# Seven products for every tile pair of the second MLP matrix, groups that alternate, and factors of twelve pairs made during the convolution

## The chip, the core and the metric

One core of one Trainium2 chip runs the whole program. The metric is the device time of one execution in microseconds (us). The kernel before took 1999.94 us, the median of three runs (1997.73 to 2001.57).

## What is computed

Two decoder layers over 256 tokens of width 2048, in float32. Layer 0 mixes with a gated short convolution, layer 1 with multi-head latent attention; each has a squared-ReLU MLP with 8192 hidden columns. The change lies in the MLP's second matrix, and uses the convolution's time.

In short:

```python
def short_conv_mixer(x, w_in, conv_w, w_out):
    gate_b, gate_c, u = jnp.split(x @ w_in, 3, axis=-1)
    y = causal_conv(gate_c * u, conv_w)          # width 3
    return (gate_b * y) @ w_out

def sq_relu_mlp(x, w1, w2):
    return jnp.square(jax.nn.relu(x @ w1)) @ w2

for layer in range(2):
    h = layer_norm(ALPHA * h + mix, ln_g[layer, 0], ln_b[layer, 0])
    h = layer_norm(ALPHA * h + sq_relu_mlp(h, mlp_w1[layer], mlp_w2[layer]),
                   ln_g[layer, 1], ln_b[layer, 1])
```

## The kernel before

**Numbers in two parts.** Every operand is kept as a high part, rounded to the matrix engine's float32r type, and a low part, the rest. `split` (L125 to L128) makes both from one 128x1024 tile: ScalarE casts the high part (L127), VectorE subtracts it from the source for the low part (L128). A product of two such operands is three matmuls: high by high, high by low, low by high (`dot`, L297 to L303).

**The stream of weights.** All weights pass once through a list `stream`, in the order in which the matrix engine needs them. `prepare` (L141) loads an entry from DRAM into one or more of five `raws` buffers of 128x1024 (`RAW`, on SyncE's queue, L138) and splits it into `hi` and `lo` tiles, of which there are eight each (`WA`). `take` (L183) hands an entry to the matrix engine and issues the preparation of what lies up to five steps ahead (`LOOK`). A plain entry is one step; an entry of the fast kind is three.

**The MLP.** It runs in eight passes `q` over 1024 hidden columns each. The first half of a pass (called W1 below) makes eight blocks of 128 hidden columns, `ps_u`, each from two 128x1024 tiles of the first matrix and 16 matmuls by the high part (512 columns) and 16 by the low part (256 columns), L215 and L219. The helper `hidden` brings each block through ReLU and square and splits it. The second half (W2) multiplies these eight hidden blocks by 1024 rows of the second matrix. Its 2048 output columns are two groups `g` of 1024; each group takes the hidden blocks in four pairs `j`, so a pass has eight (group, pair) steps.

**The fast kind.** In passes 1 to 6 (`FAST`) a pair is a 2x2 product of blocks (two halves of the tokens by two hidden blocks; two hidden blocks by two halves of the group's columns) in the form that needs seven products instead of eight. `FACTORS` (L340) lists them in order: 3, 1, 5, 7, 2, 6, 4. On the side of the hidden blocks the sums S1 to S4 are made by `form` (L703). On the side of the weights the entry loads two tiles, r1 (blocks 11 and 22) and r2 (21 and 12), and VectorE makes four derived blocks: T1 and T3 in one subtraction of 1024 columns (L162), T2 (L166) and T4 (L169) in one of 512 each. Then r1, the tile with T1 and T3, r2 (now 21 and T2), and T4 are split. T1 is used first by product 5, 21 by product 2, T4 by product 4. Beside the four output blocks of a group the form keeps four more sums (`OWN`: 1, 5, 7, 6), in `sums`; `fold` (L669) adds them into the outputs in the last pass.

**"sssp".** `MIXED` (L38) says that group 1, which always comes first, has three fast pairs and one plain pair: two plain entries of the stream, eight products, with an output sum of its own, "22". Group 0 has four fast pairs. So 57 products a pass.

**Sums between passes.** The sums of a group live in SBUF between uses. Group 1's eight are copied by ScalarE into PSUM banks during W1 (`resume` L626, through `resumed` L612) and back after W2's first group (`put_back` L616). Of group 0's seven, four are copied in before that group and back after it; for products 2, 6 and 4 it starts from nothing, and VectorE adds the result into SBUF (`keep`, L624), 128x512 each. In layer 1 passes 1 to 4 also add a block of the residual (`turn_residual`, two VectorE operations a pass).

**Order of the work.** The order of each engine's instructions is made by a planner that simulates the program at build time; each engine then runs its own list in that order and waits where a semaphore is not yet there. So the list can place preparation of weights between other work, but not change when something is late.

## Time and profile before

| what | value |
|---|---|
| median of three runs | 1999.94 us (1997.73 to 2001.57) |
| span of the profiled execution | 1994.9 us |
| matrix engine (PE) busy | 1987.7 us, 100% |
| VectorE (DVE) busy | 1709.4 us, 86% |
| ScalarE (ACT) busy | 1354.9 us, 68% |
| transfers | 385.85 MB, mean 193 GB/s |
| convolution, input products | until about 272 us |
| MLP of layer 0, passes 1 to 6 | 452.8 to 953.1 us |
| MLP of layer 1, passes 1 to 6 | 1395.4 to 1897.4 us |

The span runs from the first to the last instruction that the profiler records; the time of a run is some 5 us longer. A matmul's recorded duration overlaps the next one's, so the spacing of starts tells the pace. Busy time of VectorE in a stretch counts overlapping records once.

### The profile page before, as it was taken

The page shows a single profiled execution, that of the slowest core. Times are in us where ns is not written, and L with a number is a line of the kernel's source. Part 1 is how long each engine was busy: PE and PEld are TensorE (multiplying, and loading weights), DVE is VectorE, ACT ScalarE, POOL GpSimd, SP SyncE. Part 2 cuts the span into 40 slices and gives each one's busy share as a digit, 9 for nine tenths or more (in the row PEclk, how much of TensorE's full clock was granted, in tenths as well). Part 3 has the DMA queues.
Part 4 walks back from the last instruction along what each step waited for, and adds up shares of the span by engine and source line. Part 5 has one row for each costly group of instructions (what it writes and reads, how often), then busy time and mean ns, then how long its engine had stood idle before and what let it go on. Part 6 is the DMA issues. An engine that isn't in the chain of part 4 may idle for free.

```text
span 1994.9 us, 30180 instructions
## 1 busy us (share of the span) xinstructions
PE 1987.7 (100%) x11110; PEld 1737.2 (87%) x11110; DVE 1709.4 (86%) x2555; ACT 1354.9 (68%) x2154; POOL 2.3 (0%) x21
## 2 busy tenths in 40 slices
PE   9999999999999999999999999999999999999998
PEld 8888888988888888888889998898888888888886
DVE  8667667797999989989978988777899999999985
ACT  6444445586778778777756755558677787887772
POOL 0000000000000000000000000000000000000000
PEclk9999999999999999999999999999999999999999
DMA  8666666565657466574855543656464656656483
GB/s 318 205 191 187 190 190 190 179 193 157 212 170 251 148 216 221 177 243 147 281 171 159 170 140 123 201 180 195 146 233 155 232 161 220 222 178 233 150 269 130
DMA packets 106853, 385.85 MB, mean 193 GB/s; under 512 B 11857, under 2 KB 12625, under 8 KB 106449
## 3 DMA queue, kind: packets, MB, share of 16 engines
q1 hardware_dynamic: 106560, 383.79, 59.5%
q8 instruction: 87, 1.43, 0.3%
q14 instruction: 62, 0.50, 0.1%
q10 hardware_dynamic: 144, 0.13, 0.0%
HBM read 381.78 MB, written 2.10 MB: 192 GB/s over the span
## 4 chain that ended last, share of the span: by engine, by line
PE 98%; DVE 1%; ACT 1%; issue 0%; DVEq 0%; ACTq 0%
PE ps_u L215 20%; PE ps_l L215 13%; PE ps_u L219 10%; PE ps_l L219 7%; PE ps_f L300 4%; PE ps_f L303 4%; PE ps_f L302 4%; PE ps_r L303 4%; PE ps_r L302 4%; PE ps_r L300 4%; PE ps_d L300 2%; PE ps_d L302 2%; PE ps_d L303 2%; PE ps_w L249 2%; PE ps_w L248 2%; PE ps_w L247 2%
## 5 line engine op out<-in xcount | busy, mean ns | idle before, releaser
L128 DVE TENSOR_TENSOR lo<-raw,hi 128x1024 fp32r<-128x1024 f32 x710 | 861.8, 1220 | 190.6 <-ACT hi L127 119.9
L127 ACT CAST hi<-raw 128x1024 fp32r<-128x1024 f32 x710 | 741.8, 1051 | 247.4 <-PE ps_l L215 98.1
L215 PE MATMUL ps_u<-xhl,hi 128*128 128x512 f32 x1792 | 621.7, 392 | 0.0
L219 PE MATMUL ps_u<-xhl,lo 128*128 128x256 f32 x1792 | 498.2, 279 | 0.0
L215 PEld LDWEIGHTS ps_u<-xhl,hi 128*128 128x128 f32 x1792 | 334.5, 187 | 73.6 <-ACT acc L595 0.2
L219 PEld LDWEIGHTS ps_u<-xhl,lo 128*128 128x128 f32 x1792 | 338.1, 189 | 1.8
L215 PE MATMUL ps_l<-xhl_a,hi 128*128 128x512 f32 x704 | 244.1, 393 | 0.0
L219 PE MATMUL ps_l<-xhl_a,lo 128*128 128x256 f32 x704 | 195.4, 279 | 0.0
L215 PEld LDWEIGHTS ps_l<-xhl_a,hi 128*128 128x128 f32 x704 | 132.1, 188 | 29.9
L219 PEld LDWEIGHTS ps_l<-xhl_a,lo 128*128 128x128 f32 x704 | 131.9, 188 | 0.2
L127 ACT CAST hi_t<-raw_t 128x1024 fp32r<-128x1024 f32 x84 | 88.5, 1054 | 45.8 <-DVE raw_t L162 41.4
L162 DVE TENSOR_TENSOR raw_t<-raw,raw 128x1024 f32<-128x1024 f32 x84 | 102.3, 1218 | 1.8 <-DMA raw<-in_w2f_dram 1.5
L128 DVE TENSOR_TENSOR lo_t<-raw_t,hi_t 128x1024 fp32r<-128x1024 f32 x84 | 102.4, 1219 | 0.2
L718 ACT ACTIVATE fp<-fp 128x256 f32<-128x256 f32 x96 | 40.0, 416 | 63.2 <-DVE fp L356 62.6
L215 PE MATMUL ps_l<-z,hi 128*128 128x512 f32 x240 | 82.4, 391 | 0.0
L300 PE MATMUL ps_d<-hi,h 128*128 128x512 f32 x192 | 75.0, 391 | 0.0
L302 PE MATMUL ps_d<-lo,h 128*128 128x512 f32 x192 | 75.0, 390 | 0.0
L303 PE MATMUL ps_d<-hi,h 128*128 128x512 f32 x192 | 74.8, 389 | 0.0
L249 PE MATMUL ps_w<-xd,hi 128*128 128x258 f32 x256 | 72.7, 284 | 0.0
L248 PE MATMUL ps_w<-xd,lo 128*128 128x258 f32 x256 | 72.3, 282 | 0.0
L247 PE MATMUL ps_w<-xd,hi 128*128 128x258 f32 x256 | 72.3, 282 | 0.0
L215 PE MATMUL ps_l<-oT,hi 128*128 128x512 f32 x208 | 71.3, 391 | 0.0
(296 smaller groups left out, 3963.7 us busy)
## 6 DMA issues: line engine op xcount, KB each, us to landing
raw<-in_w_dram SPq DMA_DIRECT2D x344, 512.0 KB, 4.5
raw<-in_w2f_dram SPq DMA_DIRECT2D x168, 512.0 KB, 3.9
raw<-in_w_in_dram SPq DMA_DIRECT2D x88, 512.0 KB, 4.2
raw<-in_w_out_dram SPq DMA_DIRECT2D x32, 512.0 KB, 3.7
raw<-in_w_o_dram SPq DMA_DIRECT2D x32, 512.0 KB, 4.2
raw<-in_w_kv_dram SPq DMA_DIRECT2D x10, 512.0 KB, 3.7
raw<-in_w_q_dram SPq DMA_DIRECT2D x8, 512.0 KB, 4.0
raw<-in_w_uk_dram SPq DMA_DIRECT2D x8, 512.0 KB, 3.9
```

The costliest lines, as they stand in the source:

```text
L127: nc.scalar.copy(hi, src)
L128: nc.vector.tensor_tensor(lo, src, hi.bitcast(F32), ALU.subtract)
L162: nc.vector.tensor_tensor(t.rearrange(two, a=2), b12.unsqueeze(1).to_broadcast([P, 2, BW]), r1.rearrange(two, a=2), ALU.subtract)
L215: nc.tensor.matmul(ps, w[blk // 8][0][:, blk % 8, :], x, start=first, stop=False)
L219: nc.tensor.matmul(ps[:, :T], w[blk // 8][1][:, blk % 8, :], x[:, :T], start=False, stop=last)
L247: nc.tensor.matmul(ps[:, :W], hi, x[k][:, :W], start=k == 0, stop=False)
L248: nc.tensor.matmul(ps[:, :W], lo, x[k][:, :W], start=False, stop=False)
L249: nc.tensor.matmul(ps[:, :W], hi, x[k][:, W:], start=False, stop=k == NC - 1)
L300: nc.tensor.matmul(ps, x[0], w[0], start=first, stop=False, skip_group_check=onto)
L302: nc.tensor.matmul(ps[:, at], x[0], w[1][:, at], start=False, stop=False, skip_group_check=onto)
L303: nc.tensor.matmul(ps, x[1], w[0], start=False, stop=last, skip_group_check=onto)
L718: nc.scalar.activation(f, f, AF.Relu)
```

## The change

All eight pairs of a pass are of the fast kind, in both layers: `MIXED` goes, and the plain pair's two entries become one fast entry. A pass has 56 products.

The groups alternate: pass 1 takes group 1 and then group 0, pass 2 group 0 and then group 1, and so on (`groups`). The group that ends a pass begins the next one. Its products 3, 1, 5 and 7 stay in their PSUM banks over the pass boundary; 2, 6 and 4 are copied back and in again (`end`, `first_sums`). Between the two groups of a pass each bank changes hands product by product: in the first group's last pair, as soon as a product is done, `turn` copies its sum back and copies the second group's next sum into the bank that came free. All sums now go through `resumed` and `put_back` on ScalarE; `keep` on VectorE goes.

For layer 0 alone, two of a pass's eight entries (the third pair of the first group and the second pair of the second group, `EARLY`) get their derived blocks from DRAM. During the convolution's loop over `m` the generator `making` loads r1 and r2 of one such entry on GpSimd's DMA queue, and in the next turn VectorE makes T1, T3, T2 and T4 with the same three subtractions, and two DMAs on the same queue write them to a DRAM tile: 12 entries, at `m` from 1 to 13. In the MLP such an entry then is four loads (r1, the tile T1 T3, the tile T2 T4, and block 21 of 256 KB) and no subtraction but those of the splits.

The residual blocks of layer 1 are added in the order 0, 2, 1, 3.

```diff
-MIXED = "sssp"
-EVEN = (QC - 1, "22")
+EARLY = {0: ((0, 2), (1, 1))}
...
+    def groups(q):
+
+        return (1, 0) if (q - FAST[0]) % 2 == 0 else (0, 1)
+
+    stored = ctx.enter_context(tc.tile_pool(name="stored", bufs=1, space=bass.MemoryType.DRAM))
+    made = {}
+    for l, q in [(l, q) for l in EARLY for q in FAST]:
+        for i, j in EARLY[l]:
+            t = stored.tile([2, P, 1024], F32, tag=f"m{l}_{q}_{i}_{j}", name=f"made{l}_{q}_{i}_{j}")
+            made[l, q, i, j] = (t[0], t[1])
...
-            for j, kind in enumerate(MIXED):
-                out += [(w2f[l, q, 1, j, 0], w2f[l, q, 1, j, 1])] if kind == "s" else \
-                    halves(w2[l, q, 2, j]) + halves(w2[l, q, 3, j])
-            out += [(w2f[l, q, 0, j, 0], w2f[l, q, 0, j, 1]) for j in range(QC // 2)]
+            for i, g in enumerate(groups(q)):
+                for j in range(QC // 2):
+                    out.append((w2f[l, q, g, j, 0], w2f[l, q, g, j, 1]) + made.get((l, q, i, j), ()))
...
+    def making(l, pool):
+
+        for (k, q, i, j), (to13, to24) in made.items():
+            if k != l:
+                continue
+            name = f"{l}_{q}_{i}_{j}"
+            r1, r2, t = (pool.tile([P, 1024], F32, tag=g, name=f"{g}{name}") for g in ("m1", "m2", "m3"))
+            for r, src in zip((r1, r2), w2f[l, q, groups(q)[i], j]):
+                nc.gpsimd.dma_start(r, src)
+            yield
+            b22, (b21, b12) = r1[:, BW:], (r2[:, :BW], r2[:, BW:])
+            two = "p (a c) -> p a c"
+            nc.vector.tensor_tensor(t.rearrange(two, a=2), b12.unsqueeze(1).to_broadcast([P, 2, BW]),
+                                    r1.rearrange(two, a=2), ALU.subtract)
+            nc.vector.tensor_tensor(r1[:, :BW], b22, t[:, :BW], ALU.subtract)
+            nc.vector.tensor_tensor(r1[:, BW:], b21, r1[:, :BW], ALU.subtract)
+            nc.gpsimd.dma_start(to13, t)
+            nc.gpsimd.dma_start(to24, r1)
...
+        def fourth(src):
+            f = state["fast"].tile([P, 2, BW], F32R, tag="t4", name=f"t4_{i}", bufs=2)
+            split(f[:, 0, :], f[:, 1, :], src)
+            return [f[:, 0, :], f[:, 1, :]]
+
+        def named(names):
+            return {n: [v.rearrange("p b c -> p (b c)")[:, o:o + BW] for v in w]
+                    for w, pair in zip(out, names) for n, o in zip(pair, (0, BW))}
+
+        if len(stream[i]) == 4:
+            r1, t13 = load_raw(f"{i}_0", stream[i][0]), load_raw(f"{i}_1", stream[i][2])
+            finished(r1, f"{i}_1")
+            yield
+            t24 = load_raw(f"{i}_2", stream[i][3])
+            b21 = raws.tile([P, 1024], F32, tag="raw", name=f"raw{i}_3")[:, :BW]
+            nc.sync.dma_start(b21, stream[i][1][:, :BW])
+            finished(t13, f"{i}_t")
+            yield
+            finished(t24, f"{i}_2")
+            ready[i] = {**named((("11", "22"), ("T1", "T3"), ("T2", "T4"))), "21": fourth(b21)}
+            yield
+            return
...
+    making_in = ExitStack()
+    before_mlp = making(0, making_in.enter_context(tc.tile_pool(name="making0", bufs=2)))
...
+        if m:
+            next(before_mlp, None)
+    making_in.close()
...
+        def first_sums(ps, banks, m):
+
+            g = groups(q)[0]
+            for p in {0: ("3", "1", "5", "7") if q == FAST[0] else (), 4: "2", 5: "6", 6: "4"}.get(m, ()):
+                banks.setdefault(p, busy[m % 4])
+                ps[p] = resumed(p, g, f"ps_r{p}", banks[p])
...
-        def keep(p, g, ps):
-
-            at = place(p, g)
-            if q == FAST[0] and p in OWN:
-                nc.scalar.copy(at, ps)
-            else:
-                nc.vector.tensor_tensor(at, at, ps, ALU.add)
...
+            order = [p for p, _, _ in FACTORS]
+            after, place_of = {}, {}
+
+            def begin_next(p, bank):
+                after[p], place_of[p] = resumed(p, second, f"ps_f{p}", bank), bank
+
+            def turn(p):
+                put_back(p, first, ps[p])
+                i = order.index(p) + 1
+                if i < len(order):
+                    begin_next(order[i], banks[p])
+
+            def end(p):
+                if q == FAST[-1] or p not in order[:4]:
+                    put_back(p, second, after[p])
+
             for j in range(n):
-                fast_products(then, h, forms, j, set(then) - onto if j == 0 else (), then if j == n - 1 else (), onto)
-            for p, _, _ in FACTORS:
-                (put_back if p in onto or p in new else keep)(p, 0, then[p])
-            return (b3, b1, b5, b7), (b6, b2, b4, b22)
+                if j == n - 1:
+                    begin_next(order[0], spare)
+                fast_products(ps, h, forms, j, new if j == 0 else (), ps if j == n - 1 else (), set(ps) - new,
+                              turn if j == n - 1 else None)
+            stay = order[:4] if q < FAST[-1] else []
+            for j in range(n):
+                fast_products(after, h, forms, j, new if j == 0 else (), after if j == n - 1 else (),
+                              set(order) - new, end if j == n - 1 else None)
+            if stay:
+                return [banks[order[-1]]] + [place_of[p] for p in order[4:]], {p: after[p] for p in stay}, \
+                    {p: place_of[p] for p in stay}
+            return [banks[order[-1]]] + [place_of[p] for p in order[:3]], {}, {p: place_of[p] for p in order[3:]}
...
-        busy, free = (0, 1, 2, 3), (4, 5, 6, 7)
+        busy, sums_in, places = (0, 1, 2, 3), {}, {"3": 4, "1": 5, "5": 6, "7": 7}
```

More of the change, by code (lines that the diff above doesn't have):

```diff
@@ new lines, in down_pairs @@
+        def down_pairs(h, forms, ps, banks, spare):
+            first, second = groups(q)
+            new = set(OWN) if q == FAST[0] else set()
+            n = QC // 2
+            order = [p for p, _, _ in FACTORS]
[10 more added lines that the diff above has]
+                    put_back(p, second, after[p])
+            for j in range(n):
+                if j == n - 1:
[10 more added lines that the diff above has]
+            return [banks[order[-1]]] + [place_of[p] for p in order[:3]], {}, {p: place_of[p] for p in order[3:]}
@@ L748, in mlp @@
                         for t in range(2):
-                            extra(block, q - 1, t, busy[2 + t])
+                            extra(block, (0, 2, 1, 3)[q - 1], t, busy[2 + t])
                     if q in FAST:
-                        resume(busy, free, begun, m)
+                        first_sums(sums_in, places, m)
                     if q == NQ - 1:
@@ L773, in mlp @@
             else:
-                busy, free = down_pairs(h, forms, busy, free, begun)
+                busy, sums_in, places = down_pairs(h, forms, sums_in, places, busy[3])
     def to_wide(block, put, h):
```

47 lines of the change are left out of this document (6 added, 41 removed).

## The prediction

> **What bounds the kernel now.** First the page's head, its slices and its chain of waits.
>
> ```profile
> span 1994.9 us, 30180 instructions
> PE 1987.7 (100%) x11110; PEld 1737.2 (87%) x11110; DVE 1709.4 (86%) x2555; ACT 1354.9 (68%) x2154; POOL 2.3 (0%) x21
> ...
> PE   9999999999999999999999999999999999999998
> ...
> DVE  8667667797999989989978988777899999999985
> ...
> PE 98%; DVE 1%; ACT 1%; issue 0%; DVEq 0%; ACTq 0%
> ```
>
> The matrix engine never stops, and 98% of the chain is its own. But VectorE is at nine tenths through both MLPs, so I read busy time by stretch next: a W2 of layer 0, a W2 and the W1 after it in layer 1, the opening, the convolution.
>
> ```profile
> core 0: us, PE busy (x) PEld busy (x) DVE busy (x) ACT busy (x) POOL busy (x), PEclk, DMA share, GB/s
> 497.20:536.00 38.80, 38.80 (x174) 32.12 (x173) 38.48 (x47) 30.09 (x43) 0.00 (x0) 1.00 0.52 172
> ...
> 1439.80:1478.80 39.00, 39.00 (x175) 32.33 (x174) 38.66 (x47) 30.30 (x43) 0.00 (x0) 1.00 0.53 166
> 1478.80:1523.20 44.40, 44.40 (x261) 38.94 (x260) 40.15 (x58) 35.19 (x57) 0.00 (x0) 1.00 0.62 213
> ...
> 0.00:30.00 30.00, 28.95 (x162) 25.89 (x163) 22.44 (x50) 22.43 (x51) 0.34 (x6) 1.00 0.90 339
> 30.00:272.00 242.00, 242.00 (x1394) 212.29 (x1393) 165.08 (x245) 112.20 (x149) 1.39 (x14) 1.00 0.65 200
> ```
>
> Through a whole W2 VectorE works 38.66 of 39.00 us: there both engines are full at once. In W1 it has 4.25 us to spare. So the question is how late VectorE may be at the end of a W2, where it prepares the last pair. Here are its instructions at the end of pass 6 in layer 1, the low part of T1/T3 first (columns: start, duration), then of pass 1 in layer 1, and of passes 1 and 6 in layer 0.
>
> ```profile
> 1892.32 1.22 DVE L128 TENSOR_TENSOR lo_t<-raw_t,hi_t 128x1024 fp32r<-128x1024 f32 x1
> 1893.45 1.22 DVE L128 TENSOR_TENSOR lo<-raw,hi 128x1024 fp32r<-128x1024 f32 x1
> 1894.59 0.69 DVE L128 TENSOR_TENSOR t<-raw,t 128x512 fp32r<-128x512 f32 x1
> 1895.19 2.35 DVE L128 TENSOR_TENSOR lo<-raw,hi 128x1024 fp32r<-128x1024 f32 x2
> 1897.46 0.68 DVE L624 TENSOR_TENSOR acc<-acc,ps_f 128x512 f32<-128x512 f32 x1
> ...
> 1472.24 1.22 DVE L128 TENSOR_TENSOR lo_t<-raw_t,hi_t 128x1024 fp32r<-128x1024 f32 x1
> ...
> 529.85 1.22 DVE L128 TENSOR_TENSOR lo_t<-raw_t,hi_t 128x1024 fp32r<-128x1024 f32 x1
> ...
> 948.19 1.22 DVE L128 TENSOR_TENSOR lo_t<-raw_t,hi_t 128x1024 fp32r<-128x1024 f32 x1
> ```
>
> And the matrix engine's first matmul of product 4 in the last two pairs of pass 6, and in the last pair of the other three.
>
> ```profile
> 1891.94 0.39 PE L300 MATMUL ps_f<-t,h 128*128 128x512 f32 x1
> 1896.70 0.39 PE L300 MATMUL ps_f<-t,h 128*128 128x512 f32 x1
> ...
> 1477.97 0.39 PE L300 MATMUL ps_f<-t,h 128*128 128x512 f32 x1
> ...
> 535.32 0.39 PE L300 MATMUL ps_f<-t,h 128*128 128x512 f32 x1
> ...
> 952.38 0.39 PE L300 MATMUL ps_f<-t,h 128*128 128x512 f32 x1
> ```
>
> A pair, seven products, takes 1896.70 - 1891.94 = 4.76 us, so a product 0.68 us. Product 5 is the first to need T1 and comes four products, 2.72 us, before product 4: at 1893.98. Its low part is there at 1892.32 + 1.22 = 1893.54. The **margin** is 0.44 us. In pass 1 of layer 1 it is 1.79 us. The six passes of layer 1 give 1.79, 1.45, 1.00, 0.69, 1.27, 0.44, mean 1.11; those of layer 0 1.53, 0.70, 1.83, 0.44, 0.97, 0.25 (first and last above), mean 0.95. Low part of r2 and T4 come behind with a little more to spare.
>
> The starts above also give VectorE's pace: 1.135 us for 1024 columns, 0.60 us for 512, one behind the other.
>
> **The change, part by part.** *One product fewer a pass.* 12 passes x 0.68 = 8.2 us off the matrix engine, and the only gain on the path: 0.68 us a pass.
>
> *The plain pair becomes a fast one.* Plain: two splits, 2 x 1.135 = 2.27 us of VectorE. Fast: three splits and the T1/T3 subtraction, 4 x 1.135, and three operations of 512 (T2, T4, split of T4), 3 x 0.60: 6.34 us. So 4.07 us more in each W2, ahead of the last pair. ScalarE gets one and a half casts more; it has 8 us free in a W2.
>
> ```profile
> L162 DVE TENSOR_TENSOR raw_t<-raw,raw 128x1024 f32<-128x1024 f32 x84 | 102.3, 1218 | 1.8 <-DMA raw<-in_w2f_dram 1.5 <-DVE lo L128 0.3
> L127 ACT CAST hi<-raw 128x1024 fp32r<-128x1024 f32 x710 | 741.8, 1051 | 247.4 <-PE ps_l L215 98.1 <-DMA raw<-in_w_dram 29.9 <-PE ps_d L303 27.9
> L616 ACT COPY sums<-ps_r 128x512 f32<-128x512 f32 x48 | 25.6, 586 | 23.2 <-PE ps_r L303 23.2
> ```
>
> A rule speaks for a higher price. The Trainium skill, "VectorE: DVE Perf Modes", section "The TRN2 errata", gives a float32 two-operand operation (N + 151)/0.96 ns, that is 1.22 and 0.69 us, and a latency that is exposed between instructions; the sum by it would be 4.52 us a pass, and layer 1 2.7 us later than below. The durations in the rows agree with the formula, but the starts are 1.13 and 0.60 us apart, so I go by the starts.
>
> *Layer 1.* VectorE has no gap in W2, so the 4.07 us arrive whole at the last pair, less the margin. The matrix engine's pass grows by 4.07 less the margin (the saved product is swallowed: it would only wait earlier). Mean 4.07 - 1.11 = 2.96; six passes +17.8 us. `keep` leaves, 3 x 0.60 = 1.8 us, but it lies behind the last pair (1897.46 above), and pays back that VectorE then enters W1 later by its lost margin. Can the 4.25 us free in W1 start the pairs earlier? What bounds that is the eight buffers and the order of work: casts already wait there for the matrix engine to release a buffer.
>
> ```profile
> ACT hi L127 <- PE ps_u L215: 27.3, 31, 1.8
> ...
> 540.27 1.23 DVE L128 TENSOR_TENSOR lo<-raw,hi 128x1024 fp32r<-128x1024 f32 x1 [1.41 <-ACT hi L127]
> 541.74 1.23 DVE L128 TENSOR_TENSOR lo<-raw,hi 128x1024 fp32r<-128x1024 f32 x1 [0.25 <-ACT hi L127]
> ```
>
> Bounds: if less work in W1 gives every pass the margin of pass 1, 6 x (4.07 - 1.79) = +13.7; if none has more than pass 6, 6 x 3.63 = +21.8. I take +17.8, the margins as they stand.
>
> *Layer 0, made factors.* Each made entry saves the three subtractions, 1.135 + 2 x 0.60 = 2.34 us; two save 4.67, against 4.07 added: 0.60 us less in W2. If that is all, the margin stays (0.60 less for VectorE, 0.68 less for the matrix engine), and layer 0 gains 6 x 0.68 = 4.1 us. But a made entry takes four of the five `raws` buffers and does only about one split per load. A buffer that comes free is usable again after the load and the cast:
>
> ```profile
> raw<-in_w2f_dram SPq DMA_DIRECT2D x168, 512.0 KB, 3.9
> ```
>
> 3.9 + 1.05 = 4.95 us. Behind an ordinary pair, which holds three buffers, the third load starts when that pair's T1/T3 is split; until its low part can start VectorE has r2's split, T4's, and two of the made entry, 1.135 + 0.60 + 2 x 1.135 = 4.0 us: a gap of 0.95, and likewise about 1.05 before the next pair's r1. So up to 2.0 us for the entry in the second group; the one in the first lies behind the last hidden block's work and costs less. Also the T1/T3 subtraction of the first group's third pair, done before W2 begins today, is no head start any more: up to 1.14. Worst: -0.60 + 2.0 + 1.14 - 0.95 = +1.6 a pass, +9.5 in all. The nearest row is the run of single loads in W1 just shown, where VectorE loses about 0.25 us per load: four loads 1.0 us, and half the head start 0.6: +0.05 a pass. I take 0 for layer 0, bounds -4.1 and +9.5.
>
> *Making them.* 12 x 2.34 = 28 us of VectorE in a stretch where it is free for 77 of 242 us, at most 2.34 us in one turn of some 17 us, while weights lie ahead; without that cover it would cost those 28 us. The GpSimd queue also carries each turn's two-column memset, behind stores whose data were due a turn earlier. Transfers: per entry two loads and two stores of 0.52 MB, 25 MB in 210 us, 120 GB/s on top of 200. The opening moved 339 GB/s; 200 GB/s at share 0.65 would mean a limit of 308. Bounds 0 and 320/308 of 210 us, 8 us; I take 0, by the opening's row. The Trainium skill, "DMA: Bandwidth & Descriptors", "Issuing engines are not separate DMA queues", says that transfers from any queue share the same 16 engines, and "Where 436 GB/s comes from" a limit of about 358 GB/s per core at the memory; by it the sum stays at 0.
>
> *Copies at the change of groups.* 13 copies (seven back, six in) between the end of product 3 in the first group's last pair and the use of product 4 in the next pair, thirteen products or 8.9 us later. At some 0.5 us each they take 6.5; with one pair's casts between (three of 1.05 and one of 0.6, 3.6) 10.1: up to 1.2 us late. In layer 1 that hides in VectorE's delay; in layer 0 it is 0 to +7. Some ten such copies stand at the same place today without stopping the matrix engine; I take 0. `resume`'s eight copies in W1 become three.
>
> *Sum.* 17.8 + 0 + 0 + 0 = +17.8: span 1994.9 + 17.8 = 2012.7, and the median lies 5.0 us above the profiled span: **2017.7 us**. The terms' bounds, 13.7 - 4.1 and 21.8 + 9.5, give this case's own range: 2009 to 2031.
>
> **Rivals.**
> 1. *The matrix engine stays the bound* (faster): over a whole pass of layer 1 VectorE needs 38.66 + 40.15 + 4.07 - 1.8 = 81.1 us, the matrix engine 83.4 - 0.7 = 82.7. If the planner moves the pairs' preparation 2.3 to 3.6 us earlier into W1, nothing waits: -8.2, 1991.8. It decides at T1's low part of the last pair. Against it: the buffers.
> 2. *Half of that*: W1, freed of `keep`, gives a head start of 1.8 us beyond pass 1's margin: layer 1 6 x (4.07 - 1.79 - 1.8) = +2.9, layer 0 -4.1: 1998.7, no change.
> 3. *Made factors don't relieve VectorE*: buffers eat what the subtractions saved, +9.5: 2027. For it the waits on loads in W1; against it the planner's freedom to interleave.
> 4. *ScalarE late at the change of groups* in layer 0, +7: 2025.
> 5. *The convolution's transfers at their limit*, +8: 2026.
> 6. *All margins as in pass 1, layer 0 free*: +9.6, 2009.5.
>
> **How the numbers follow.** Forecast 0.40; rivals 1: 0.16, 2: 0.09, 3: 0.14, 4: 0.07, 5: 0.05, 6: 0.09. A measurement here tells about 0.2%, 4 us, from no change. Faster is rival 1, 0.16; same rival 2, 0.09; slower the rest, 0.75. The range leaves out rival 1 and a little on top: 1996 to 2031.
>
> **What would show it.** In layer 1 the last pair's T1/T3 low part ends after product 5 could have begun, and the matrix engine idles some 3 us near the end of each W2, waiting for L128; W2 lengthens from 38.8 to about 41.8 us; layer 0's stays at 38.1. VectorE's busy time grows by about 12 x 4.07 less `keep`, some 27 us (the made subtractions only move). Wrong: if layer 1's W2 takes 38.1 us, the pairs were prepared earlier, and rival 1 holds; if layer 0's lengthens, 3 or 4; if the convolution does, 5.

## The result, and the profile after

The changed kernel takes **2076.29 us** (median of four, 2074.37 to 2081.53) against 1999.25 us (1997.73 to 2001.57): 1.039 times as long, 95% interval 1.0375 to 1.0405. Forecast were 2017.7 us and a range of 1996 to 2031. The side was right; the loss is four times the forecast one.

The head, GpSimd's slices and the chain of waits of the changed kernel's page:

```profile
span 2072.6 us, 30201 instructions
PE 2023.3 (98%) x11062; PEld 1728.8 (83%) x11062; DVE 1738.2 (84%) x2581; ACT 1356.5 (65%) x2142; POOL 28.2 (1%) x69
...
POOL 1120000000000000000000000000000000000000
...
PE 68%; DVE 14%; DMA 7%; ACT 7%; issue 5%; DVEq 0%; SPq 0%; POOL 0%; ACTq 0%; POOLq 0%
```

Of the chain the matrix engine kept 98% before; now a third of it belongs to VectorE, ScalarE, transfers and issue. VectorE has 28.8 us more to do, near the 27 forecast. So the extra work is as counted, and what was mis-sized is what the engines wait for. GpSimd is a first sign: its row is used up after three slices of 52 us, where the change's text spreads its transfers over turns 1 to 13.

Busy time by stage shows where the 77.7 us of span came from. Before: opening and convolution up to the end of its input products; the six fast passes of layer 0; those of layer 1.

```profile
0.00:272.90 272.90, 271.85 (x1561) 239.04 (x1562) 188.42 (x294) 135.44 (x201) 1.73 (x20) 1.00 0.68 216
...
452.78:953.06 500.28, 499.82 (x2569) 427.49 (x2568) 467.02 (x603) 391.65 (x602) 0.00 (x0) 1.00 0.59 194
...
1394.56:1897.38 502.82, 502.82 (x2601) 430.06 (x2600) 471.30 (x611) 392.01 (x601) 0.00 (x0) 1.00 0.59 193
```

The same three stretches after:

```profile
0.00:294.10 294.10, 278.99 (x1562) 243.48 (x1563) 213.07 (x330) 133.91 (x201) 27.64 (x68) 0.98 0.83 286
...
473.93:1004.40 530.47, 513.90 (x2545) 421.55 (x2544) 457.79 (x584) 394.67 (x596) 0.00 (x0) 1.00 0.61 201
...
1445.92:1974.19 528.27, 516.46 (x2577) 423.10 (x2576) 488.80 (x628) 392.65 (x595) 0.00 (x0) 1.00 0.56 184
```

The convolution grew by 21.2 us, layer 0 by 30.2, layer 1 by 25.45; the stretches between them are equal to 0.1 us, and the tail is 0.9 longer. Forecast were 0, 0 and 17.8. In layer 0 VectorE even has 9 us *less* to do than before, and the stage is 30 us longer: there it is not the amount of VectorE's work that sets the time. Nor is all of the growth idle time: in layer 0 the matrix engine is idle for 16.6 us and in the first stage for 15.1, and the rest is matmuls that follow each other more slowly.

Inside these stages: first, from before, the 125 us behind the opening; then, after, the opening, the same 125 us, the rest of the convolution, a W2 of layer 0 and one of layer 1. Each W2 runs here to its last matmul; one matmul of the next W1 lies inside.

```profile
30.00:155.00 125.00, 125.00 (x722) 109.65 (x721) 85.44 (x124) 59.11 (x78) 0.80 (x8) 1.00 0.67 211
...
0.00:30.00 30.00, 24.10 (x121) 21.28 (x122) 20.25 (x48) 17.00 (x42) 4.74 (x14) 0.89 0.95 369
30.00:155.00 125.00, 115.79 (x640) 100.13 (x640) 91.01 (x129) 49.43 (x68) 22.11 (x46) 0.97 0.96 346
155.00:294.00 139.00, 139.00 (x803) 121.97 (x802) 101.70 (x154) 67.37 (x93) 0.80 (x8) 1.00 0.69 214
605.70:649.20 43.50, 40.72 (x172) 30.93 (x170) 36.68 (x43) 31.92 (x46) 0.00 (x0) 1.00 0.54 171
1577.70:1620.40 42.70, 40.89 (x171) 30.65 (x169) 40.97 (x49) 31.65 (x46) 0.00 (x0) 1.00 0.43 145
```

The matrix engine stands still in the first 155 us only, and the convolution's rest runs as before. About a third of the loss falls in the opening (121 matmuls against the 162 that the prediction's row shows), two thirds in the 125 us behind it (640 against 722). Part of it is a lower clock: the granted clock was 0.89 and 0.97 there, where the kernel before had 1.00, so that nearly the same number of matmuls keeps the engine busy for 279.0 us in place of 271.9. In layer 1's W2 (last row) VectorE is busy for 40.97 of the 42.70 us: the picture forecast. In layer 0's it is idle for 6.8 of 43.5 us, and the matrix engine still stands for 2.8.

Where layer 1's W2 stops, the matrix engine and then VectorE in the timeline (start, duration; in brackets the idle time before and what ended it):

```profile
1614.77 0.40 PE L348 MATMUL ps_f<-hi,h 128*128 128x512 f32 x1
1616.07 0.73 PE L345 MATMUL ps_f<-hi_t,forms 128*128 128x512 f32 x2 [0.90 <-ACT hi_t L154]
...
1613.72 1.22 DVE L211 TENSOR_TENSOR raw_t<-raw,raw 128x1024 f32<-128x1024 f32 x1
1614.97 0.69 DVE L215 TENSOR_TENSOR raw<-raw,raw_t 128x512 f32<-128x512 f32 x1
...
1616.30 1.22 DVE L155 TENSOR_TENSOR lo_t<-raw_t,hi_t 128x1024 fp32r<-128x1024 f32 x1
```

The last pair's T1 and T3 are subtracted until 1614.94 (L211, before L162), ScalarE casts them, and the matrix engine, whose last matmul of product 1 ends at 1615.17, waits 0.90 us for that cast (L154, before L127). The place is the forecast one, product 5 of the last pair. But what it waits for is one step earlier than forecast, the high part and not VectorE's low part. It isn't the only stop: in layer 1's six W2s the matrix engine is idle for 6.2 us in six such waits, and for 4.9 us in 22 shorter ones, for casts and low parts of the second group's pairs.

Where layer 0's VectorE idles, the group of T1/T3 subtractions over the whole run, and the worst wait of the W2 above:

```profile
L211 DVE TENSOR_TENSOR raw_t<-raw,raw 128x1024 f32<-128x1024 f32 x84 | 102.4, 1220 | 28.1 <-DMA raw<-in_w2f_dram 27.9
...
632.56 1.23 DVE L211 TENSOR_TENSOR raw_t<-raw,raw 128x1024 f32<-128x1024 f32 x1 [3.53 <-DMA raw<-in_w2f_dram]
```

As many subtractions waited 1.5 us for loads before; now 27.9 us, of which 25.2 fall between 474 and 1005 us. That is VectorE's idle time, and not yet time that the matrix engine loses. What the matrix engine waits for is told by the table of waits for the same stretch (us in total, times, longest):

```profile
DVE raw_t L211 <- DMA raw<-in_w2f_dram: 25.2, 19, 3.9
PE ps_f L345 <- ACT hi_t L154: 6.3, 6, 1.7
PE ps_f L345 <- ACT ps_f L671: 4.7, 6, 1.2
```

Beside the wait at product 5 it waits once in each of the six W2s for a sum that ScalarE copies in at the change of groups (L671). In the trace that copy stands on ScalarE behind four casts in a row, the last of them the made tile's T1 and T3.

And the convolution. First the making's subtraction of 1024 columns, then GpSimd's first issue of loads, its last load and its last store:

```profile
L121 DVE TENSOR_TENSOR m<-m,m 128x1024 f32<-128x1024 f32 x12 | 14.7, 1223 | 34.3 <-DMA m<-in_w2f_dram 27.8 <-issue 6.5
...
1.33 1.71 POOL L117 DMA_DIRECT2D m<-in_w2f_dram  x3 [0.46 <-issue]
...
140.37 0.53 POOL L117 DMA_DIRECT2D m<-in_w2f_dram  x1 [4.74 <-DMA made<-m]
...
152.26 0.53 POOL L126 DMA_DIRECT2D made<-m  x1 [3.60 <-DVE m L124]
```

The three first loads are issued at 1.33 us, amid the loads of the opening, and the last store at 152 us, two thirds of the way to the turn in which the loop over `m` asks for it. The planner took them forward: nothing in the code ties a load to its turn. VectorE waits 34.3 us at the head of its queue, with the convolution's own splits behind it.

### The profile page after: what moved, and what is told of

The parts are those of the page before. It is cut to its first block, busy times and chain, and to the rows that moved or that the text cites. A ratio compares the mean times of both kernels' runs of the same rounds, so it can differ in the third digit from the quotient of the medians.

```text
span 2072.6 us, 30201 instructions
## 1 busy us (share of the span) xinstructions
PE 2023.3 (98%) x11062; PEld 1728.8 (83%) x11062; DVE 1738.2 (84%) x2581; ACT 1356.5 (65%) x2142; POOL 28.2 (1%) x69
## 3 DMA queue, kind: packets, MB, share of 16 engines
q8 instruction: 87, 1.43, 0.3%
## 4 chain that ended last, share of the span: by engine, by line
PE 68%; DVE 14%; DMA 7%; ACT 7%; issue 5%; DVEq 0%; SPq 0%; POOL 0%; ACTq 0%; POOLq 0%
PE ps_u L260 13%; PE ps_l L260 12%; PE ps_u L264 7%; PE ps_l L264 6%; DVE lo L155 5%; DMA raw<-in_w2f_dram 4%; ACT hi L154 3%; DVE raw_t L211 2%; PE ps_d L345 2%; PE ps_d L347 2%; PE ps_d L348 2%; DMA raw<-in_w_dram 2%; PE ps_f L347 2%; PE ps_f L348 2%; PE ps_w L294 2%
## 5 line engine op out<-in xcount | busy, mean ns | idle before, releaser
L154 ACT CAST hi<-raw 128x1024 fp32r<-128x1024 f32 x710 | 740.0, 1049 | 319.4 <-PE ps_l L260 70.7
L260 PE MATMUL ps_u<-xhl,hi 128*128 128x512 f32 x1792 | 628.9, 396 | 0.0
L260 PEld LDWEIGHTS ps_l<-xhl_a,hi 128*128 128x128 f32 x704 | 133.6, 190 | 30.2
L154 ACT CAST hi_t<-raw_t 128x1024 fp32r<-128x1024 f32 x84 | 88.4, 1052 | 61.8 <-DVE raw_t L211 49.9
L211 DVE TENSOR_TENSOR raw_t<-raw,raw 128x1024 f32<-128x1024 f32 x84 | 102.4, 1220 | 28.1 <-DMA raw<-in_w2f_dram 27.9
L345 PE MATMUL ps_f<-hi_t,forms 128*128 128x512 f32 x176 | 68.2, 405 | 15.9 <-ACT hi_t L154 12.5
```

Source lines behind the costliest of these rows:

```text
L154: nc.scalar.copy(hi, src)
L211: nc.vector.tensor_tensor(t.rearrange(two, a=2), b12.unsqueeze(1).to_broadcast([P, 2, BW]), r1.rearrange(two, a=2), ALU.subtract)
L260: nc.tensor.matmul(ps, w[blk // 8][0][:, blk % 8, :], x, start=first, stop=False)
L345: nc.tensor.matmul(ps, x[0], w[0], start=first, stop=False, skip_group_check=onto)
```

## The experiments

Two theories stood at the start. **A**: three separate causes, the making's place in time (+21), VectorE at its limit in the W2s (layer 1 and, without made factors, layer 0 alike), and load buffers that eat what made factors save. **B**, in several forms: bandwidth in the convolution, or the copies at the change of groups, or some effect of the made entries that reaches all stages. "Layer 0" and "layer 1" below are the six passes; the kernel before has 500.28 and 502.82 us.

**Without the made factors.** Everything else of the change stays.

```diff
-EARLY = {0: ((0, 2), (1, 1))}
+EARLY = {}
```

> All pairs fast and groups alternating, but no factors are made ahead (the table of early entries is empty). Theory A (VectorE bounds each W2; the making costs the convolution 21 us; made entries bring layer 0 nothing, because their loads wait for buffers): the convolution ends at 273 us as before, layer 0's six passes take about as long as layer 1's, some 25 us over before, so about 2050 us. Rival B (the made entries do relieve layer 0, only not enough): layer 0 gets slower without them, by up to 2 x 2.34 us a pass, 28 us in all: the passes of layer 0 grow by some 55 us instead of 30, about 2080 us.

2049.86 us, ratio 1.0259 (1.0244 to 1.0274). The convolution is as before (452.65 us at the start of layer 0's passes), layer 1 grows by 23.7 us, and layer 0 takes 526.2 us without made factors and 530.5 with them. So the twelve made entries bring nothing where they are used. The T1/T3 subtractions of this kernel, twelve more than above, and the matrix engine's waits for copied sums in layer 0:

```profile
L211 DVE TENSOR_TENSOR raw_t<-raw,raw 128x1024 f32<-128x1024 f32 x96 | 116.9, 1218 | 4.7 <-DMA raw<-in_w2f_dram 4.0 <-DVE fp L403 0.2
...
PE ps_f L345 <- ACT ps_f L671: 0.9, 2, 0.6
```

VectorE waits 4.0 us for loads against 27.9, and the matrix engine 0.9 us for copied sums in layer 0 against 4.7. Both come with the made entries. The wait at product 5 is the same with and without them (6.3 and 6.2 us), so the copies' 3.8 us are nearly all of the 4.3 by which layer 0 is worse with made factors.

**The making alone.** To the kernel before, `making` and its calls are added as in the change; what it makes isn't used.

```diff
+EARLY = {0: ((0, 2), (1, 1))}
...
+    making_in = ExitStack()
+    before_mlp = making(0, making_in.enter_context(tc.tile_pool(name="making0", bufs=2)))
...
+        if m:
+            next(before_mlp, None)
+    making_in.close()
```

> The kernel before, to which only the making during the convolution is added, its results unused. Theory A (the making alone costs the convolution 21 us, and the MLPs' loss is separate): 1999 + 21 = 2020 us. Rival B (the convolution suffers from something else in the change, such as another order of the weights' loads): 1999 to 2005 us.

2020.28 us, ratio 1.011 (1.0095 to 1.0125). The two parts give +51.4 and +21.8 us, 73 of the 77, and the rest is the 4 us by which the made entries are worse than none.

**The making's transfers alone.** As before, without the three subtractions and the tile that they wrote (`to13` is written from r2).

```diff
-            nc.vector.tensor_tensor(t.rearrange(two, a=2), b12.unsqueeze(1).to_broadcast([P, 2, BW]),
-                                    r1.rearrange(two, a=2), ALU.subtract)
-            nc.vector.tensor_tensor(r1[:, :BW], b22, t[:, :BW], ALU.subtract)
-            nc.vector.tensor_tensor(r1[:, BW:], b21, r1[:, :BW], ALU.subtract)
-            nc.gpsimd.dma_start(to13, t)
+            nc.gpsimd.dma_start(to13, r2)
```

> The kernel before with the making's transfers alone: r1 and r2 of twelve pairs are loaded and stored on GpSimd's queue as early as buffers allow, and VectorE does none of the subtractions. With the subtractions this was 2020 us. Theory A (VectorE's waiting for the loads is the larger part): 2000 to 2008 us. Rival B (the transfers delay the opening's and the convolution's own loads): 2013 to 2022 us.

2009.34 us, ratio 1.0056 (1.0041 to 1.0071), between the two. Its opening and its next 125 us:

```profile
0.00:30.00 30.00, 21.30 (x99) 18.37 (x100) 13.82 (x38) 14.17 (x37) 5.81 (x16) 0.96 0.93 363
30.00:155.00 125.00, 125.00 (x719) 109.59 (x718) 87.25 (x126) 62.30 (x85) 21.09 (x46) 1.00 0.99 390
```

All of the loss lies in the opening: 99 matmuls where the kernel before has 162, at 0.17 us each some 11 us. The first weights' 1 MB loads land after 19.4 us instead of 11.2. Behind that, the same transfers run at 390 GB/s and the matrix engine never stops. So volume costs nothing there. By the difference of the two runs, half of the 21 us is the opening's loads delayed, and the other half comes with the subtractions, behind whose waits VectorE's other work stands. The halves aren't the same stretches of time in both runs: here no store waits for VectorE, the transfers come earlier, and the opening suffers more than in the changed kernel, where the first loads land after 15.6 us.

**The loads held to their turn.** ScalarE writes a column of the load's tile from a value that the turn computes, so the load can't go ahead of it. `state["turn"]` is set to `y[:, :1]` in the loop over `m`.

```diff
             for r, src in zip((r1, r2), w2f[l, q, groups(q)[i], j]):
+                nc.scalar.copy(r[:, :1], state["turn"])
                 nc.gpsimd.dma_start(r, src)
```

> The changed kernel, but the loads of each made entry are held to their turn of the convolution's loop: ScalarE first copies one column of that turn's result into each buffer, so that the load cannot be issued earlier. Theory A (the 21 us come from the planner's pulling all twelve entries into the first 152 us, where transfers run at 346 GB/s and weights come late): spread out, demand is some 320 GB/s over 200 us and the convolution loses 0 to 8 us; total about 2055 to 2063. Rival B (it is the volume, or the GpSimd queue and VectorE's work itself, wherever it stands): still about +21 us, 2076.

2088.45 us, ratio 1.0461 (1.0436 to 1.0485): worse than the change itself, and against both expectations. The subtraction of 1024 columns in this kernel:

```profile
L122 DVE TENSOR_TENSOR m<-m,m 128x1024 f32<-128x1024 f32 x12 | 14.7, 1225 | 77.8 <-issue 62.4 <-DMA m<-in_w2f_dram 15.3
```

The load now waits for its turn, but VectorE's order still has the subtraction early, so VectorE stands at it for 77.8 us in all, and the convolution takes 34.7 us more than before. That made a sharper claim: not the transfers' place alone matters but the place of the waiting instruction in VectorE's order.

**Loads and subtraction held.** To the kernel just shown, a column of the subtraction's target is written from the next turn's value too.

```diff
+            nc.scalar.copy(t[:, :1], state["turn"])
             nc.vector.tensor_tensor(t.rearrange(two, a=2), b12.unsqueeze(1).to_broadcast([P, 2, BW]),
                                     r1.rearrange(two, a=2), ALU.subtract)
```

> Like the gated run (2088 us), but the three subtractions are held back as well, by one turn of the loop (ScalarE first copies a column of the next turn's result into the tile that the first subtraction writes), so that the loads have some 16 us. Theory A (in the convolution VectorE stands at the head of its queue behind a subtraction whose loads on GpSimd's queue have not landed; 62 + 15 us of such waits in the gated run, 28 in the changed kernel): these waits go, the convolution loses 0 to 8 us instead of 30 to 33, total 2055 to 2063. Rival B (the volume of transfers delays the weights wherever it stands): 2070 to 2088.

2052.76 us, ratio 1.0269 (1.0253 to 1.0284). The subtraction, and the windows of the convolution behind the opening:

```profile
L123 DVE TENSOR_TENSOR m<-m,m 128x1024 f32<-128x1024 f32 x12 | 14.6, 1219 | 0.0
...
30.00:155.00 125.00, 125.00 (x721) 109.64 (x720) 98.49 (x142) 61.24 (x99) 14.83 (x34) 1.00 0.89 311
155.00:273.00 118.00, 118.00 (x682) 103.56 (x681) 93.77 (x141) 55.10 (x89) 12.34 (x28) 1.00 0.85 294
```

No wait, and the matrix engine full all through: layer 0's passes begin at 453.18 us, 0.4 later than in the kernel before. The 28 us of VectorE and the 25 MB are indeed hidden, once they come in their turns. (This run moves both causes at once, the transfers out of the opening and the subtractions behind their loads; that each counts is shown by the run of transfers alone and by the gated one.)

**VectorE's price by itself.** In the kernel before, the T4 subtraction is done twice: 0.60 us for each of seven pairs, 4.2 us of VectorE a pass, with no change to copies or products.

```diff
         nc.vector.tensor_tensor(t4, b21, b12, ALU.subtract)
+        nc.vector.tensor_tensor(t4, b21, b12, ALU.subtract)
```

> The kernel before, with T4's subtraction done twice in each of its seven fast pairs: 7 x 0.60 = 4.2 us more of VectorE in each W2, nothing else. Theory A (4.07 us more of VectorE in W2 is all that the MLPs lose by): each pass grows by 4.2 less its margin, mean 1.03 us, and a little more for what follows the stalls: 12 x 3.2 = +38, and up to +50: 2037 to 2050 us. Rival B (the alternating groups and their copies are what costs): 1998 to 2010 us.

2030.56 us, ratio 1.016 (1.0143 to 1.0177), 6 us under the lower end for VectorE as the bound, and far from the rival's. Layer 1 grows by about 17 us and layer 0 by about 15, without the 2 us of the next W1's matmuls that here run ahead of each stage's last ones. By the prediction's formula, 4.2 less the margin, layer 1 would grow by 6 x (4.2 - 1.11) = 18.5 and layer 0 by 6 x (4.2 - 0.95) = 19.5: near for layer 1, some 5 us too much for layer 0, for a cause that stays open.

**VectorE relieved.** The kernel without made factors, and without the T2 and T4 subtractions: 8 x 2 x 0.60 = 9.6 us of VectorE a pass less.

```diff
-        nc.vector.tensor_tensor(b12, b22, t[:, :BW], ALU.subtract)
         finished(r2, f"{i}_2")
         t4 = r1[:, :BW]
-        nc.vector.tensor_tensor(t4, b21, b12, ALU.subtract)
```

> As the run without made entries, but the two 512-column subtractions for T2 and T4 are left out of every fast pair in both layers, so products 6 and 4 take other blocks as factors; loads, casts, splits, copies and matmuls stay. VectorE has 8 x 1.2 = 9.6 us less to do in each W2. Theory A (VectorE alone sets the pace of W2): the stalls of some 4.4 us a pass vanish in all twelve passes, and the matrix engine's saving shows: 1999 - 8 = 1991 us. Rival B (ScalarE's 13 copies at the change of groups, or the buffers for loads, set it): most of the 50 us stay, 2030 us or more.

1997.78 us, ratio 0.9995 (0.9986 to 1.0004): 52 us less than with them, so VectorE's lateness is what the MLPs of that kernel pay for. But it isn't the gain of 8.2 us that twelve products would give. The only longer waits of the matrix engine that are left in the MLPs are two in layer 1, 1.1 us in all and up to 0.86, for sums that ScalarE copies in (`resumed`).

**And without the copies at the change of groups.** The first group's sums aren't put back there, and the second group starts from nothing; the sums are cleared once in each MLP.

```diff
+        nc.gpsimd.memset(sums, 0.0)
...
-                after[p], place_of[p] = resumed(p, second, f"ps_f{p}", bank), bank
+                after[p], place_of[p] = psum(f"ps_f{p}", bank), bank
...
-                put_back(p, first, ps[p])
...
-                fast_products(after, h, forms, j, new if j == 0 else (), after if j == n - 1 else (),
-                              set(order) - new, end if j == n - 1 else None)
+                fast_products(after, h, forms, j, order if j == 0 else (), after if j == n - 1 else (),
+                              (), end if j == n - 1 else None)
```

> The run without T2 and T4 (1997.8 us, though the matrix engine has 8.2 us less to do) without the copies at the change of groups too: the first group's sums are not copied back, the second group's start from nothing, so 13 copies of ScalarE a pass go, and with them any wait of the second group's products for a bank; the sums are cleared once per MLP so that the later folding reads defined values. Theory A (ScalarE's copies there cost the remaining 0.35 us or more a pass): W2 falls from some 38.5 to 38.15 us and the time to 1991 to 1994 us. Rival B (the rest lies elsewhere, such as in the first pass's start or the last W1): 1996 to 1999 us.

1988.73 us, ratio 0.9944 (0.9927 to 0.996): 9 us less than with the copies, and below the expectation. A W2 of layer 1, with the copies and then without:

```profile
1607.76:1646.56 38.80, 38.53 (x171) 31.28 (x169) 33.65 (x37) 31.81 (x47) 0.00 (x0) 1.00 0.47 159
```

```profile
1601.94:1640.05 38.11, 38.11 (x170) 31.54 (x169) 34.56 (x38) 25.83 (x33) 0.00 (x0) 1.00 0.58 179
```

38.11 us are 56 products of 0.68 and not a wait. The product saved is really worth 0.68 us a pass, but only with both VectorE's T2 and T4 and ScalarE's copies out of the way. Of the 9 us, layer 1's passes give 4.1 and layer 0's 3.0.

**T4 on GpSimd**, which is idle in the MLP, in the kernel without made factors.

```diff
-        nc.vector.tensor_tensor(t4, b21, b12, ALU.subtract)
+        nc.gpsimd.tensor_tensor(t4, b21, b12, ALU.subtract)
```

> As the run without made entries (2050 us), but T4's subtraction, 128x512, runs on GpSimd in all fast pairs: 8 x 0.60 = 4.8 us less on VectorE in each W2, about what it is late there. If GpSimd's work costs VectorE nothing, the stalls go and the time is near that of the run without T2 and T4, 1998 to 2004 us. If GpSimd holds VectorE back while it reads SBUF, or is itself some us late with T4, most of the 50 us stay: 2030 us or more.

2095.33 us, ratio 1.0486 (1.047 to 1.0502), 45 us slower than on VectorE. The subtraction, and VectorE's low part of T1 and T3 beside it:

```profile
L218 POOL TENSOR_TENSOR raw<-raw 128x512 f32<-128x512 f32 x96 | 137.7, 1434 | 1578.4 <-DMA raw<-in_w2f_dram 716.5 <-DVE lo L155 411.2 <-DVE raw L215 238.2
...
L155 DVE TENSOR_TENSOR lo_t<-raw_t,hi_t 128x1024 fp32r<-128x1024 f32 x96 | 137.3, 1430 | 17.5 <-ACT hi_t L154 17.5
...
1625.75 2.20 DVE L155 TENSOR_TENSOR lo_t<-raw_t,hi_t 128x1024 fp32r<-128x1024 f32 x1 [0.39 <-ACT hi_t L154]
...
PE ps_f L345 <- ACT ps_f L671: 30.5, 12, 3.9
ACT t L154 <- POOL raw L218: 27.1, 57, 1.9
```

GpSimd takes 1.43 us where VectorE takes 0.69, and VectorE's own operation rises from 1.22 us to 1.43 in the mean, up to 2.20. The Trainium skill, "SBUF — State Buffer", section "SBUF: two separate sides", says that a VectorE operation with two operands from this memory and a GpSimd operation that reads it exclude each other for a whole instruction; 1.22 us with part of 1.43 waited agrees with that. But the last two lines, waits over the whole run, show a larger price than VectorE's stretching: ScalarE stands 27.1 us in 57 waits for GpSimd's T4, the copies stand behind those casts, and the matrix engine stands 30.5 us in twelve waits for copied sums, where the kernel without this edit has 0.9 in two. Behind such long stops the clock fell too: the granted clock was 0.97 and 0.98 in the two layers' passes, 1.00 without the edit.

**A sixth raw buffer.** `RAW` becomes 6, and to make room the tile of T4's parts has one buffer in place of two. In the changed kernel:

```diff
-RAW, WA = 5, 8
+RAW, WA = 6, 8
...
-            f = state["fast"].tile([P, 2, BW], F32R, tag="t4", name=f"t4_{i}", bufs=2)
+            f = state["fast"].tile([P, 2, BW], F32R, tag="t4", name=f"t4_{i}", bufs=1)
```

> The changed kernel with six buffers for raw weights instead of five; the memory for it comes from T4's split, which has one buffer instead of two. Theory A (layer 0's made entries bring nothing because their four loads find no free buffer, so that the next pair's r2 comes late): layer 0 gets faster by some of the 25 us of waits for loads in its passes, 8 to 20 us more than the kernel without made entries gains from the same edit. Rival B (something else holds layer 0): both gain alike, within 4 us.

2063.16 us, ratio 1.0319 (1.0304 to 1.0335), 13.1 us less than the change. The same edit in the kernel without made factors:

> The kernel without made entries (2050 us) with six raw buffers and one for T4: the control for the run before it. Its pairs hold three buffers and wait little for loads, so theory A says 2045 to 2055 us; if one buffer for T4 holds VectorE back, it is slower than 2055, and the pair of runs says so.

2046.94 us, ratio 1.0241 (1.0224 to 1.0258): 2.9 us less than without the edit. So 10 us of the 13 belong to the made entries, as theory A has it. Layer 0 falls from 530.5 to 519.3 us with them, from 526.2 to 523.9 without. VectorE's wait isn't gone, though. In the third W2 of layer 0 (from 694 us in the changed kernel, up to the next W1's first matmul) three waits of 4.1 us together become one of 2.9, and the W2 takes 39.8 us in place of 41.3. Over layer 0's six passes the same two rows as above, and the one at product 5, read with six buffers:

```profile
DVE raw_t L211 <- DMA raw<-in_w2f_dram: 21.2, 9, 3.4
PE ps_f L345 <- ACT hi_t L154: 3.6, 5, 0.8
```

VectorE's waits for loads fall by 4.0 us only. What the matrix engine loses falls by more: 2.7 us at product 5, and the row of waits for copied sums, 4.7 us, is gone. The clock drop at the end of layer 0's pass 6 (below), 1.7 us, is gone as well. So the buffers reach the matrix engine in good part by way of ScalarE's order, and VectorE's 25 us of waits are a poor measure of the price.

**All that helped, together**: loads and subtraction held to their turns, and six buffers.

> The changed kernel with both repairs: loads and subtractions of the making held to their turns (the convolution then lost under 1 us) and six raw buffers with one for T4 (which gave 13 us with made entries and 3 without). If the two add up: 2076.3 - 23.5 - 13.1 = about 2040 us. If the repairs overlap, 2045 to 2053. Under 2000 only if VectorE were not the bound of layer 1.

2040.81 us, ratio 1.0201 (1.0186 to 1.0216). With the making hidden and a sixth buffer the made factors at last bring 6 us against the kernel without them, but no version that computes all the sums came out below the kernel before.

## Why the prediction was right, and where it failed

**Layer 1** (forecast +17.8, bounds 13.7 and 21.8; measured +25.45). The mechanism is the forecast one: both engines full in W2, four more microseconds of VectorE, the longest stop at product 5 of the last pair. Doubled T4 confirms the size of that part, about 17 us against 18.5 by the same working. The failed step is in *Copies at the change of groups*: "In layer 1 that hides in VectorE's delay". It doesn't hide, because VectorE itself waits for it. In the W2 shown above:

```profile
1603.34 0.62 ACT L671 COPY ps_f<-acc 128x512 f32<-128x512 f32 x1
1603.86 1.08 ACT L154 CAST hi<-raw 128x1024 fp32r<-128x1024 f32 x1
...
1604.97 1.22 DVE L155 TENSOR_TENSOR lo<-raw,hi 128x1024 fp32r<-128x1024 f32 x1 [0.98 <-ACT hi L154]
```

The cast of a pair's tile stands on ScalarE behind the last of the copies, and VectorE idles 0.98 us for it; in passes 2 to 5 it is 0.98, 0.99, 0.99 and 0.71, 3.7 us in all, and the kernel before has no such wait in any W2 of these passes. Without made factors, where layer 1 grows by 23.7 us, the same wait stands at the same place (0.99). The copies cost layer 1 4.1 us where VectorE isn't in the way, so the two add up. The prediction's own sum, "up to 1.2 us late", had the size; taking it as hidden was the mistake. Of the rest, 1.7 us is the clock drop shown below, which the kernel without made factors didn't have, and about 1.4 the wider spacing of W1's matmuls, also below. What remains stays open.

**Layer 0** (forecast 0, bounds -4.1 and +9.5; measured +30.2). Two steps failed. The first is the working of the gaps, in *Layer 0, made factors*: 0.95 and 1.05 us a W2, "up to 2.0 us for the entry", and then a value near 0 by the run of single loads in W1. In passes 2 to 5 the W2s measure 4.1 to 4.7 us of VectorE waiting for loads, 25.2 us in the stage. A W1's loads, one tile and one split each, were the wrong row: an entry's T1/T3 subtraction needs both its tiles, and these come last behind a made entry's four. So rival 3's mechanism, "buffers eat what the subtractions saved", is there, with too low a price. The second is the 0 for the copies, rival 4's mechanism with its +7: the matrix engine is idle 4.7 us for copied sums in layer 0, 0.9 without made factors. Without them layer 0 takes 26 us more than before, so most of the +30.2 isn't the made factors' doing: it is the price of the eighth fast pair and the copies, which the made factors were to pay and didn't. The sixth buffer takes 11 us off the stage, with the matrix engine's waits as above. Why VectorE's wait of some 3 us a W2 stays with six is open.

**The convolution** (forecast 0, bounds 0 and 8; measured +21.2). The quantity argued about was right: 28 us of VectorE and 25 MB fit, as the version with both held shows, at 311 and 294 GB/s without a stop. What failed is the unspoken premise of "at most 2.34 us in one turn of some 17 us", that work written into a turn is done in that turn. The planner moved all of it into the first 152 us. There it delayed the opening's loads, and set VectorE waiting in order for loads that took 7 us; by the run of transfers alone each is about half. Rival 5 had the place right, and a part of the cause, transfers that delay weights, but in the opening and not over the whole stretch.

**The product saved**, 8.2 us, was right as a term, and as one that is swallowed: only the kernel without T2, T4 and copies shows it. **The copies** at 0 were wrong by what the prediction's own working bounded for layer 0, 0 to +7: without T2 and T4 they cost 7.1 us over both layers' passes. (In that working three casts of 1.05 us and one of 0.6 make 3.75 us and not 3.6, which changes nothing.)

**What would show it.** W2 of layer 1 was to rise from 38.8 to 41.8 us; it takes 41 to 43, and 45 in pass 6. W2 of layer 0 was to stay at 38.1: it rose, which was named as the sign of rival 3 or 4, and both have a part in it. The convolution grew, named as that of rival 5. So the signs were well chosen. But the three zeros, each taken by the favourable row, were not independent: all supposed that new work fits where its engine has time free, without asking what it stands behind, or in front of, in that engine's order.

## What to carry to other kernels

Before pricing extra work as hidden, ask what ties it to its place: a planned order can take anything without a dependency forward, and an instruction that waits at the head of an in-order engine can cost more than its own time or its bytes, because what stands behind it is late too. If it has to be held, hold the consumer as well as the load; here holding the load alone was worse than not holding it. An engine that is idle for a fifth of the time isn't free either: thirteen copies in one lump made the casts behind them late, and casts in front of them made the copies late. And work taken off a full engine by loading its result can move the wait to the buffers of the load, so count how many buffers each entry holds, and for how long, before counting what it saves.

## What the runs showed of the hardware

**A clock that falls after a short stop.** In pass 6 of layer 1 of the changed kernel the matrix engine waited for a cast; the matmuls behind it, and the window (the clock is the column after GpSimd's):

```profile
1966.52 0.40 PE L348 MATMUL ps_f<-hi,h 128*128 128x512 f32 x1
1968.56 0.73 PE L345 MATMUL ps_f<-hi_t,forms 128*128 128x512 f32 x2 [1.64 <-ACT hi_t L154]
...
1970.94 0.63 PE L347 MATMUL ps_f<-lo_t,forms 128*128 128x512 f32 x1
1971.37 0.63 PE L348 MATMUL ps_f<-hi_t,forms 128*128 128x512 f32 x1
...
1968.50:1974.20 5.70, 5.42 (x16) 4.03 (x17) 5.49 (x6) 5.22 (x9) 0.00 (x0) 0.70 0.61 175
1970.10:1973.40 3.30, 3.30 (x9) 2.65 (x8) 3.30 (x4) 2.82 (x5) 0.00 (x0) 0.50 0.74 218
```

The granted clock was 0.50 for 3.3 us (the first window's 0.70 is a mean), and matmuls came every 0.43 us instead of 0.23, which costs some 1.7 us. It began 1.5 us after the stop had ended. The same happened at the end of layer 0's pass 6, behind a stop of 1.66 us. The Trainium skill, "TensorE: Matmul & The Clock Gate", section "Part 1: The HAM clock gate", gives an idle window of about 3.4 us ahead of a throttle; here a stop of 1.64 us stood before it. Without made factors the same stop of 1.65 us, in both layers, was followed by a clock of 1.00, so this is not to be counted on either way.

**Matmuls a little further apart.** The W1 of layer 1's pass 5, before and after; the engine is busy all through, and the second window holds one matmul fewer:

```profile
1730.93:1775.32 44.39, 44.39 (x257) 39.12 (x256) 41.20 (x58) 35.76 (x57) 0.00 (x0) 1.00 0.69 234
1796.08:1841.16 45.08, 45.08 (x256) 39.15 (x256) 40.87 (x57) 34.70 (x55) 0.00 (x0) 1.00 0.71 238
```

A 512-column matmul is followed by the next after 0.236 us in place of 0.230, at the full clock and without a wait. In the changed kernel this holds for five of the six W1s of layer 0's stage and two of layer 1's, some 4 us and 1.4 us. No run shows why; those seven W1s all come behind a W2 in which the matrix engine stopped, but not every W1 behind such a W2 is slower.

**Transfers at 390 GB/s.** One core drew that over 125 us with its matrix engine never stopping. The Trainium skill, "DMA: Bandwidth & Descriptors", section "Where 436 GB/s comes from", which the prediction had weighed, gives some 358 GB/s per core at the memory; the measurement decides against that as a limit for a core by itself. The changed kernel's loads on GpSimd's queue took 7.2 us for 512 KB in the median. SyncE's took 4.7 for the convolution's own weights, and 3.9 for the same matrix later, in the MLPs, where less is moved.

**GpSimd beside VectorE.** An idle GpSimd is no free help for float32 subtractions here: the operation takes twice as long (1.43 us against 0.69), VectorE's own ones stretch (1.22 us to 1.43 for the low part of T1 and T3), and what comes late from GpSimd holds up ScalarE's order, with 30.5 us of waits of the matrix engine for copied sums behind it.
